# Gate and up of the last feed-forward's second half as seven block products of fp32 sums

## The chip, the core and the metric

The kernel runs on one core of a Trainium2 chip. The metric is the device time of one launch in microseconds. Engines are called PE (TensorE: matmuls, with their weight loads), DVE (VectorE), ACT (ScalarE), POOL (GpSimd) and SP (SyncE, which issues the transfers).

## What is computed

One inference step of a decoder with two layers, for a prompt of 1024 tokens and a sample group of 8 tokens that share all weights. D_MODEL is 1024, D_FF is 2816. Cut to what matters here:

```python
def swiglu(h, w_gu, w_down):
    gate, up = jnp.split(h @ w_gu, 2, axis=-1)
    return (jax.nn.silu(gate) * up) @ w_down

# for each layer l (a mixer of its own in each):
h = h + rmsnorm(mix, g[1])
h = h + rmsnorm(swiglu(rmsnorm(h, g[2]), w_gu[l], w_down[l]), g[3])
# after the last layer h is the output: y_prompt (1, 1024, 1024), y_sample (8, 1, 1024)
```

All data are fp32.

## The kernel before

Activations lie with the model dimension on the 128 partitions and tokens along the free dimension. The tokens are worked in two halves, `g` = 0 (512 prompt tokens) and `g` = 1 (512 prompt tokens and the 8 of the sample group, 520). A matmul of half 1 covers 260 tokens, so that its result fits a PSUM bank of 512 fp32; the two quarters lie in the two banks of one `mm` buffer.

fp32 products are made of three matmuls in the type fp32r: each operand is split into a rounded part and the difference to it (`split_to` for activations, `split_w` for weights: a cast on ACT, then a subtraction on DVE), and hi*hi, hi*lo and lo*hi are added up in PSUM. `proj` (matmuls: line 264) does this for 128 output channels over `nk` blocks of 128 input channels. `split_w` loads up to 4 such blocks of weights at a time (256 KB), with the cast in line 250 and the subtraction in line 251.

The feed-forward `ffn.part(pi)` works on a group of 5, 5, 4, 4 and 4 of the 22 blocks of 128 hidden channels (columns, below). For each column: the gate projection (8 input blocks x 3 x 2 quarters = 48 matmuls in half 1), `silu` (a clamp on DVE, Exp, Ln, Exp on ACT, a product on DVE), the up projection (48), their product, and a split of it (lines 271 and 272). Then eight down projections over the group's columns follow, added to `R` by `evac_raw` (line 403). In the last group `sq_acc` adds up the squares of the result (lines 300 to 304).

The normed input of a feed-forward comes from `out_proj.finish`: a residual and its sum of squares, `rstd_from` (a matmul with ones, line 293, then Ln and Exp), and `normed` (scale operations in line 310, then a split).

The order on each engine is not that of the source: a scheduler orders the instructions, and tiles come from pools with a fixed number of buffers, whose reuse waits for the last reader. `weave` fixes only the order in which streams are handed to it. Pools that matter here: `wraw` (5 raw weight tiles), `wspl` (5 split ones), `npool` (2; the tiles `n` of `sq_acc` and of `normed` in the last layer), `bpool` (7), `apool` (8), `cpool` (4), `xpool` (8 of each tag), and in PSUM `mmp` (2 x 2 banks), `smp` (3) and `nsp` (1).

The end of the kernel, around the change:

```python
    o1 = out_proj(1, 1, A, True)
    drain(o1.mm(b1.xo))
    weave((o1.finish(), 17), (f0.part(4), 8))
    f1 = ffn(1, 1, o1.x, True)
    weave((chain(f0.finish(False), store_y(0, f0.R), token_rows(1, o1.R)), 22), (chain(f1.part(0), f1.part(1)), 18))
    drain(f1.part(2), f1.part(3), f1.part(4), f1.finish_rows())
```

`f0` is the feed-forward of half 0 in the last layer, `f1` that of half 1. `store_y` and `token_rows` transpose results on PE through PSUM banks of `S()`; `first_half` and `finish_rows` turn the last result into rows of tokens and store them (Ln in line 525, Exp in line 526).

Of the kernel before, what the change touches and what calls it, by code (L numbers as in the profile page):

```python
# [8 lines left out]
F32 = mybir.dt.float32  # L9
# [8 lines left out]
P = 128  # L18
# [4 lines left out]
def tile_decoder(  # L23
# [38 lines left out]
    mmp = pool("mmp", 2, space=PSUM)  # L62
    smp = pool("smp", 3, space=PSUM)
    nsp = pool("nsp", 1, space=PSUM)
# [3 lines left out]
    def nm(s):  # L68
        uid[0] += 1
        return f"{s}_{uid[0]}"  # L70
# [9 lines left out]

    def NS():
        return nsp.tile([P, 512], F32, tag="ns", name=nm("ns"))
# [21 lines left out]
    def S():  # L104
        return smp.tile([P, 512], F32, tag="s", name=nm("s"))
# [209 lines left out]

    def wo_tiles(g):
        return [X(g) for _ in range(ND)]
# [89 lines left out]
    class out_proj:  # L407


        def __init__(self, g, l, store, last=False):  # L410
            self.g, self.l, self.store, self.x, self.last = g, l, store, [], last
# [11 lines left out]
        def finish(self):  # L423
            g, l = self.g, self.l
            rstd = rstd_from(self.acc, NG[g], 1.0 / D)
            acc = small([P, WID], tag="st", bufs=3)
            yield from residual(g, self.R, rstd, lambda k: gcol(l, 1, k), not self.last, acc, l == 0)
            r2 = rstd_from(acc, NG[g], 1.0 / D)
            yield
            yield from normed(g, self.R, r2, lambda k: gcol(l, 2, k), self.x, self.last)  # L430
# [23 lines left out]

    htok = []

    PARTS = [(0, 5), (5, 5), (10, 4), (14, 4), (18, 4)]

    class ffn:
# [4 lines left out]
        def part(self, pi):  # L464
# [18 lines left out]
            for m in range(ND):  # L483
                ps = proj(g, w_down[l], f0, nf, m * P, mids)
                evac_raw(g, self.R, ps, m, self.acc, pi == 0, last)
                if last and self.rows:
                    nc.scalar.activation(
                        self.R[m][:, :n], self.R[m][:, :n], AF.Copy, scale=gcol(l, 3, m)
                    )
                    if m == 3:  # L490
                        self.first_half()
# [11 lines left out]
        def first_half(self):  # L503
            self.yt = [xpool.tile([P, D], F32, tag="x0", name=nm("yT")) for _ in range(CH)]
            for c in range(CH):
                ps = S()
                for k in range(4):
                    nc.tensor.transpose(ps[:, k * P : (k + 1) * P], self.R[k][:, c * P : (c + 1) * P], ident)  # L508
                nc.scalar.copy(self.yt[c][:, :512], ps)
            self.ys = xpool.tile([P, D], F32, tag="x0", name=nm("yTs"))  # L510
            ps = S()
            for k in range(4):
                nc.tensor.transpose(ps[:NB, k * P : (k + 1) * P], self.R[k][:, G : G + NB], ident)
            nc.scalar.copy(self.ys[:NB, :512], ps[:NB, :])

        def finish_rows(self):

            ht, hsm = htok[0]
            g, R, acc = self.g, self.R, self.acc
            ps = NS()  # L520
            for c in range(CH):
                nc.tensor.matmul(ps[:, c : c + 1], acc[:, c * P : (c + 1) * P], ones[:, 0:1], start=True, stop=True)  # L522
            nc.tensor.matmul(ps[:NB, CH : CH + 1], acc[:, G : G + NB], ones[:, 0:1], start=True, stop=True)
            r = small([P, 8], tag="rr")
            nc.scalar.activation(r[:, :CH], ps[:, :CH], AF.Ln, scale=1.0 / D, bias=epsb)
            nc.scalar.activation(r[:, :CH], r[:, :CH], AF.Exp, scale=-0.5)
            rs = small([P, 8], tag="rr")
            nc.scalar.activation(rs[:NB, 0:1], ps[:NB, CH : CH + 1], AF.Ln, scale=1.0 / D, bias=epsb[:NB])
            nc.scalar.activation(rs[:NB, 0:1], rs[:NB, 0:1], AF.Exp, scale=-0.5)
            for c in range(CH + 1):  # L530
                prompt = c < CH
                n = P if prompt else NB
                yt, h = (self.yt[c], ht[c]) if prompt else (self.ys, hsm)
                rc = r[:, c : c + 1] if prompt else rs[:NB, 0:1]
                o = c * P
                pt = S()
                for k in range(4):
                    nc.tensor.transpose(pt[:n, k * P : (k + 1) * P], R[4 + k][:, o : o + n], ident)
                nc.vector.scalar_tensor_tensor(  # L539
                    yt[:n, :512], yt[:n, :512], rc, h[:n, :512], op0=ALU.mult, op1=ALU.add  # L540
                )
                nc.vector.scalar_tensor_tensor(  # L542
                    yt[:n, 512:], pt[:n, :], rc, h[:n, 512:], op0=ALU.mult, op1=ALU.add
                )
                if prompt:
                    t0 = g * G + c * P
                    nc.sync.dma_start(y_prompt[0, t0 : t0 + P, :], yt)
                else:
                    nc.sync.dma_start(y_sample.rearrange("b o d -> (b o) d"), yt[:NB])
                yield  # L550
# [689 lines left out]
```

## Time and profile before

| | us |
|---|---|
| median of 3 runs | 2550.11 |
| lowest and highest | 2548.95, 2551.8 |
| the profiled execution | 2551.36 |
| its span in the trace | 2549.6 |
| mean granted TensorE clock | 0.996 of full speed |
| first gate/up matmul of `f1` in the trace | 2144.5 after the span's start |
| last matmul of line 264 | ends at about 2535.9 |

Times in the trace are counted from the start of the span. In a row of the timeline the first number is the start, the second the length; in a row of the groups the two numbers behind the bar are the busy time of all and the mean of one in ns. A row of the windows has the busy time of PE, its weight loads, DVE, ACT and POOL, each with the count of instructions, then the granted clock, the transfers' share and GB/s.

### The profile page before, as it was taken

What the parts mean: (1) busy time and instruction counts of PE and PEld (TensorE: products, weight loads), DVE (VectorE), ACT (ScalarE), POOL (GpSimd) and SP (SyncE); (2) the same over time, 40 slices, a digit from 0 to 9 for tenths busy, and PEclk for the clock granted to TensorE, in tenths of its full rate; (3) what the DMA queues carried; (4) which work ended last, traced back from release to release, by engine and by line L of the source; (5) the groups of instructions that cost most, each with busy time, mean ns of one, the idle gap of its engine ahead of it and who ended that gap; (6) DMA issues with size and microseconds to landing.
All of it is one profiled execution on the core that took longest, in us unless ns stands there. A gap on an engine that the chain in (4) does not pass through costs nothing. (4 is left out here: it accounts for less than half of the span.)

```text
span 2549.6 us, 40536 instructions
## 1 busy us (share of the span) xinstructions
PE 2518.9 (99%) x15653; PEld 2193.2 (86%) x15653; DVE 1557.2 (61%) x2714; ACT 1186.6 (47%) x2187; POOL 43.8 (2%) x59
## 2 busy tenths in 40 slices
PE   8999999999999999999999999999999999999998
PEld 6888898878877888999999989766776798999998
DVE  6666566654775677555544577667677558444445
ACT  6346543243443445555433455455555445443334
POOL 1000000000000000000000000011000000000000
PEclk9999999999999999999999999999999999999999
DMA  6352242233644445231333445453443244323332
GB/s 186 109 162 71 75 150 76 65 112 116 182 127 129 136 153 183 86 88 57 102 93 94 126 153 179 144 153 94 135 140 115 77 124 129 110 86 103 93 92 67
DMA packets 457708, 297.91 MB, mean 117 GB/s; under 512 B 17573, under 2 KB 422642, under 8 KB 457514
## 3 DMA queue, kind: packets, MB, share of 16 engines
q1 hardware_dynamic: 454954, 286.92, 37.6%
q0 software_dynamic: 2560, 8.39, 1.1%
q8 instruction: 123, 2.02, 0.3%
q14 instruction: 71, 0.58, 0.1%
HBM read 265.44 MB, written 29.80 MB: 116 GB/s over the span
## 5 line engine op out<-in xcount | busy, mean ns | idle before, releaser
L264 PE MATMUL mm<-x,ws 128*128 128x260 f32 (+1 forms) x10080 | 1668.4, 323 | 1.4 <-ACT x L355 1.3
L264 PEld LDWEIGHTS mm<-x,ws 128*128 128x128 f32 x10080 | 1443.1, 188 | 166.3 <-issue 29.2
L250 ACT CAST ws<-w 128x512 fp32r<-128x512 f32 (+1 forms) x800 | 475.5, 595 | 878.4 <-PE mm L264 801.3
L251 DVE TENSOR_TENSOR ws<-w,ws 128x512 fp32r<-128x512 f32 (+1 forms) x800 | 523.5, 657 | 324.0 <-ACT ws L250 314.6
L264 PE MATMUL mm<-m,ws 128*128 128x260 f32 (+1 forms) x3168 | 544.4, 326 | 0.1
L264 PEld LDWEIGHTS mm<-m,ws 128*128 128x128 f32 x3168 | 455.1, 189 | 53.9 <-issue 7.1
L403 DVE TENSOR_TENSOR r<-r,mm 128x520 f32<-128x520 f32 (+1 forms) x128 | 88.3, 690 | 99.2 <-PE mm L264 97.7
L281 DVE TENSOR_SCALAR t<-mm 128x512 f32<-128x512 f32 (+1 forms) x104 | 72.1, 693 | 102.5 <-PE mm L264 102.0
L474 DVE TENSOR_TENSOR t<-t,mm 128x512 f32<-128x512 f32 (+1 forms) x88 | 60.8, 691 | 117.2 <-PE mm L264 117.2
L285 DVE TENSOR_TENSOR t<-t,t 128x512 f32<-128x512 f32 (+1 forms) x88 | 61.1, 694 | 88.3 <-ACT t L284 88.1
L304 DVE TENSOR_TENSOR st<-st,n 128x512 f32<-128x512 f32 (+1 forms) x98 | 67.0, 690 | 6.9 <-ACT n L303 5.0
L272 DVE TENSOR_TENSOR m<-t,m 128x512 fp32r<-128x512 f32 (+1 forms) x88 | 61.0, 694 | 3.7 <-ACT m L271 1.6
L282 ACT ACTIVATE t<-t 128x512 f32<-128x512 f32 (+1 forms) x88 | 55.9, 635 | 14.9 <-DVE t L281 7.8
L271 ACT CAST m<-t 128x512 fp32r<-128x512 f32 (+1 forms) x88 | 54.8, 623 | 10.1 <-DVE t L474 2.8
L283 ACT ACTIVATE t<-t 128x512 f32<-128x512 f32 (+1 forms) x88 | 55.8, 635 | 2.6
L284 ACT ACTIVATE t<-t 128x512 f32<-128x512 f32 (+1 forms) x88 | 55.9, 635 | 2.4
L902 PEld LDWEIGHTS s<-a,a 128*128 128x128 f32 x448 | 53.4, 192 | 1.2
L902 PE MATMUL s<-a,a 128*128 128x64 f32 x448 | 53.2, 271 | 0.0
L1073 PE MATMUL s<-b,trir 128*128 128x512 f32 (+3 forms) x96 | 38.0, 397 | 7.6 <-DVE b L272 5.3
L731 POOL DMA_INDIRECT c<-in_cache_sb_k,pidx x16 | 16.2, 1015 | 1640.7 <-DVE x L272 790.4
L1037 DVE SCALAR_TENSOR_TENSOR b<-b,b 128x512 f32<-128x512 f32 (+3 forms) x48 | 26.7, 556 | 28.2 <-ACT b L1036 28.0
L1085 PE MATMUL s<-b,a 128*128 128x512 f32 (+3 forms) x96 | 41.6, 515 | 1.9 <-DVE b L1040 1.5
(298 smaller groups left out, 1940.2 us busy)
## 6 DMA issues: line engine op xcount, KB each, us to landing
w<-in_w_gu SPq DMA_DIRECT2D x352, 256.0 KB, 3.0
w<-in_w_down SPq DMA_DIRECT2D x160, 256.0 KB, 2.8
w<-in_w_in_a SPq DMA_DIRECT2D x80, 256.0 KB, 2.9
w<-in_w_o SPq DMA_DIRECT2D x64, 256.0 KB, 2.8
w<-in_w_mem_kv SPq DMA_DIRECT2D x32, 256.0 KB, 2.9
c<-in_cache_mem_k SPq DMA_DIRECT2D x16, 512.0 KB, 4.2
c<-in_cache_mem_v SPq DMA_DIRECT2D x16, 512.0 KB, 3.9
w<-in_w_kv SPq DMA_DIRECT2D x32, 256.0 KB, 3.1
```

Source lines behind the costliest of these rows:

```text
L250: nc.scalar.copy(ws[:, 0, :n, :], raw[:, :n, :])
L251: nc.vector.tensor_sub(ws[:, 1, :n, :], raw[:, :n, :], ws[:, 0, :n, :].bitcast(F32))
L264: nc.tensor.matmul(ps[:, a, : PW[g]], wt, xt[k][:, xi, o : o + PW[g]], start=(k == 0 and wi == 0), stop=(k == nk - 1 and wi == 2),)
L272: nc.vector.tensor_sub(dst[1], src, dst[0].bitcast(F32))
L281: nc.vector.tensor_scalar(sv(x, g), pv(ps, g), -44.0, None, op0=ALU.max)
L282: nc.scalar.activation(d, x[:, :n], AF.Exp, scale=-1.0)
L284: nc.scalar.activation(d, d, AF.Exp, scale=-1.0)
L285: nc.vector.tensor_mul(d, d, x[:, :n])
L304: nc.vector.tensor_add(acc[:, :n], acc[:, :n], t[:, :n])
L403: nc.vector.tensor_add(dst, dst, pv(ps, g))
L474: nc.vector.tensor_mul(sv(sg, g), sv(sg, g), pv(pu, g))
L902: nc.tensor.matmul(plv[:, hh, c, :], K_[:, hh, cs], rhs, start=True, stop=True)
```

## The change

`f1` gets a class of its own, `ffn_w`. For a column, gate and up (2 output blocks) times the two halves of the 8 input blocks (0 to 3 and 4 to 7) make a 2 x 2 block matrix of weights a11, a12, a21, a22, each 128 x 512 as stored; the activations, input halves times token quarters of 260, make another. Their product is formed from seven block products (Strassen's scheme in Winograd's form) in place of eight. The sums and differences of weights (s1 to s4, fp32) are made on POOL, four of 512 elements for a column; those of the activations (r1 to r4) on POOL in `normed_w`, once. Each of the seven weight operands is then split (`split`), in place of four tiles before. Partial results are added up in single PSUM banks, with copies between banks on ACT. Silu is one activation function in place of Exp, Ln, Exp. The PSUM pools are closed ahead of `f1` and replaced by `quads`, 4 tags of 2 single banks; `S()` and `NS()` then take turns in two of these tags. Twelve small matmuls with constants are put ahead of the first column, the split weights of the later groups also use `cpool`, their raw weights `apool`, and the rates of the last `weave` are 17 to 7. `first_half` and `finish_rows` become functions without a change.

```diff
+    banks = ctx.enter_context(ExitStack())
...
+    def Q(i):
+        return single[0].tile([P, 512], F32, tag=f"q{i}", name=nm("q"))
...
     def S():
+        if single:
+            turn[0] += 1
+            return Q(3 * (turn[0] % 2))
...
+    def normed_w(R, rstd, gc, ops):
+        n, h = NG[1], PW[1]
+        xs, yt = {}, []
+        for k in range(4):
+            t0, t1 = N(), N()
+            for t, kk in ((t0, k), (t1, k + 4)):
+                nc.vector.scalar_tensor_tensor(
+                    t[:, :n], R[kk][:, :n], gc(kk), rstd[:, :n], op0=ALU.mult, op1=ALU.mult
+                )
+            x0, x1 = X(1), X(1)
+            split_to((x0[:, 0, :h], x0[:, 1, :h]), t0[:, :h])
+            split_to((x1[:, 0, :n], x1[:, 1, :n]), t1[:, :n])
+            yield
...
+            r1, r2, r3, r4 = B(), B(), B(), B()
+            nc.gpsimd.tensor_tensor(r1[:, :h], t0[:, h:n], t0[:, :h], op=ALU.subtract)
+            nc.gpsimd.tensor_tensor(r2[:, :h], t1[:, h:n], r1[:, :h], op=ALU.subtract)
+            nc.gpsimd.tensor_tensor(r3[:, :h], t1[:, h:n], t0[:, h:n], op=ALU.subtract)
+            nc.gpsimd.tensor_tensor(r4[:, :h], t1[:, :h], r2[:, :h], op=ALU.subtract)
+            zo = (k % 2) * h
+            for r, d, o in ((r1, x0, h), (r2, y, 0), (r3, y, h), (r4, z, zo)):
+                nc.scalar.copy(d[:, 0, o : o + h], r[:, :h])
+                nc.gpsimd.tensor_tensor(
+                    d[:, 1, o : o + h], r[:, :h], d[:, 0, o : o + h].bitcast(F32), op=ALU.subtract
+                )
...
+    def gate_up_w(l, f, ops, spl, whole):
...
+        a11, a12, a21, a22 = raw
+        s1, s2, s3, s4 = B(), B(), B(), B()
+        for d, x, y, op in (
+            (s1, a21, a22, ALU.add), (s2, s1, a11, ALU.subtract), (s3, a11, a21, ALU.subtract),
+            (s4, a12, s2, ALU.subtract),
+        ):
+            nc.gpsimd.tensor_tensor(d, x, y, op=op)
+
+        def split(src):
+            w = spl()
+            nc.scalar.copy(w[:, 0, :], src)
+            nc.vector.tensor_sub(w[:, 1, :], src, w[:, 0, :].bitcast(F32))
+            return w
+
+        def product(ps, src, i, first=False):
+            w = split(src)
+            for k in range(4):
+                x = ops[k][i]
+                for wi, (wj, xi) in enumerate(((0, 0), (0, 1), (1, 0))):
+                    nc.tensor.matmul(
+                        ps[:, :h], w[:, wj, k * P : (k + 1) * P], x[:, xi, :],
+                        start=(first and k == 0 and wi == 0), stop=(k == 3 and wi == 2), skip_group_check=True,
+                    )
+
+        pa, pb, pc, pd = (Q(i) for i in range(4))
+        product(pa, a11, 0, True)
+        nc.scalar.copy(pb[:, :h], pa[:, :h])
+        product(pd, s1, 4, True)
+        product(pb, s2, 5)
+        nc.scalar.copy(pc[:, :h], pb[:, :h])
+        product(pa, a12, 1)
+        sg = T()
+        nc.scalar.activation(sg[:, :h], pa[:, :h], AF.Silu)
+        product(pb, s3, 6)
+        up = T()
+        nc.scalar.copy(up[:, h:n], pd[:, :h])
+        gt = T()
+        nc.vector.tensor_add(gt[:, h:n], up[:, h:n], pb[:, :h])
+        product(pc, s4, 2)
+        nc.vector.tensor_add(gt[:, :h], up[:, h:n], pc[:, :h])
+        product(pb, a22, 3)
+        nc.scalar.activation(sg[:, h:n], gt[:, :h], AF.Silu)
+        nc.vector.tensor_mul(sg[:, :h], sg[:, :h], pb[:, :h])
+        nc.vector.tensor_mul(sg[:, h:n], sg[:, h:n], gt[:, h:n])
+        mt = M(F32R)
+        split_to((mt[:, 0, :n], mt[:, 1, :n]), sg[:, :n])
+        return mt
...
+    class ffn_w:
...
+        def spl(self):
+            self.n += 1
+            if pi_now[0] and self.n % 8 in (1, 4, 6):
+                return cpool.tile([P, 2, 512], F32R, tag="c", name=nm("ws"))
+            return wspl.tile([P, 2, 512], F32R, tag="ws", name=nm("ws"))
...
+            if pi == 0:
+                for i in (1, 2, 1, 2):
+                    ps = Q(i)
+                    for o in range(0, h, P):
+                        w = min(P, h - o)
+                        nc.tensor.matmul(
+                            ps[:, o : o + w], trir, cmpr[:, :w], start=(o == 0), stop=(o + w == h),
+                            skip_group_check=True,
+                        )
...
+            if last:
+                self.acc = small([P, WID], tag="st", bufs=3)
+                nc.scalar.preload_act_table_set("natural_log_exp_and_others")
...
-    o1 = out_proj(1, 1, A, True)
+    o1 = out_proj(1, 1, A, True, True)
     drain(o1.mm(b1.xo))
     weave((o1.finish(), 17), (f0.part(4), 8))
-    f1 = ffn(1, 1, o1.x, True)
-    weave((chain(f0.finish(False), store_y(0, f0.R), token_rows(1, o1.R)), 22), (chain(f1.part(0), f1.part(1)), 18))
+    banks.close()
+    single.append(ctx.enter_context(tc.tile_pool(name="quads", bufs=2, space=PSUM)))
+    f1 = ffn_w(1, o1.x)
+    weave((chain(f0.finish(False), store_y(0, f0.R), token_rows(1, o1.R)), 17), (chain(f1.part(0), f1.part(1)), 7))
```

In the down projections of `ffn_w` each quarter has a bank of its own and an evacuation of 260 elements, where one of 520 stood before.

More of the change, by code (lines that the diff above doesn't have):

```diff
@@ L407, in tile_decoder, with __init__ @@
     class out_proj:
[L410 to L411 removed]
+        def __init__(self, g, l, store, last=False, seven=False):
+            self.g, self.l, self.store, self.x, self.last, self.seven = g, l, store, [], last, seven
         def mm(self, xo, m0=0, m1=ND):
@@ L429, in finish @@
             yield
-            yield from normed(g, self.R, r2, lambda k: gcol(l, 2, k), self.x, self.last)
+            if self.seven:
+                yield from normed_w(self.R, r2, lambda k: gcol(l, 2, k), self.x)
+            else:
+                yield from normed(g, self.R, r2, lambda k: gcol(l, 2, k), self.x, self.last)
     def token_rows(g, R):
@@ L453, in token_rows @@
         htok.append((ht, hs_))
+    def gate_up_w(l, f, ops, spl, whole):
+        h, n = PW[1], NG[1]
+        raw = []
+        for m0 in (f * P, DFF + f * P):
+            if whole:
+                r = apool.tile([P, 2, 4, P], F32, tag="a", name=nm("w"))
+                ts = [r[:, 0], r[:, 1]]
+            else:
+                ts = [wraw.tile([P, 4, P], F32, tag="w", name=nm("w")) for _ in range(2)]
+            for i, r in enumerate(ts):
+                k0 = 4 * i
+                nc.sync.dma_start(
+                    r, w_gu[l][k0 * P : (k0 + 4) * P, m0 : m0 + P].rearrange("(k p) m -> p k m", p=P)
+                )
+                raw.append(r.rearrange("p k m -> p (k m)"))
+        a11, a12, a21, a22 = raw
[42 more added lines that the diff above has]
+        return mt
@@ L501, in finish, with first_half @@
                 yield
[L503 to L510, printed above, removed]
+    def first_half(self):
+        self.yt = [xpool.tile([P, D], F32, tag="x0", name=nm("yT")) for _ in range(CH)]
+        for c in range(CH):
@@ L511, in first_half @@
             ps = S()
             for k in range(4):
[L513 to L550, printed above, removed]
```

104 lines of the change are left out of this document (100 added, 4 removed).

## The prediction

> **What bounds the kernel now.** I read the page first (engine shares and the chain that ended last), then the windows over the last 600 us, then the timeline of PE there, and last the groups by form for prices.
>
> ```profile
> span 2549.6 us, 40536 instructions
> ...
> PE 2518.9 (99%) x15653; PEld 2193.2 (86%) x15653; DVE 1557.2 (61%) x2714; ACT 1186.6 (47%) x2187; POOL 43.8 (2%) x59
> ...
> PE 20%; DVE 0%; ACT 0%; DVEq 0%; issue 0%
> ```
> ```profile
> 2300.00:2400.00 100.00, 100.00 (x838) 100.00 (x837) 47.06 (x73) 33.70 (x57) 0.00 (x0) 1.00 0.35 100
> ```
> PE is never idle in the stage that changes: matmuls and weight loads fill this window, at the full granted clock, while DVE is busy 47%, ACT 34% and Pool not at all. A matmul taken out here is time gained, until another engine's work for it no longer fits beside the matmuls that stay.
>
> ```profile
> 2123.49 21.12 PE L264 MATMUL mm<-m,ws 128*128 128x512 f32 x90
> 2144.54 3.94 PE L264 MATMUL mm<-x,ws 128*128 128x260 f32 x31
> ...
> 2326.17 46.08 PE L264 MATMUL mm<-x,ws 128*128 128x260 f32 x384
> 2372.08 23.20 PE L264 MATMUL mm<-m,ws 128*128 128x260 f32 x192
> ```
> The changed stage begins at 2144.54, without a gap behind the last down projection of the prompt's first half. In steady state a group of four columns takes 384 gate/up matmuls from 2326.17 to 2372.08: 45.91 / 384 = 119.6 ns each, 11.48 us for a column of 96; its down projections take 23 us.
>
> **What goes.** `gate_up_w` has seven products of 12 matmuls, 84 for 96, each of the same 128x260 form, with one weight load each as before. A column takes 84 x 119.6 ns = 10.05 us of PE, a product 1.44 us. Over 22 columns 264 matmuls go: **-31.6 us**. The down projections keep theirs, and the 12 small matmuls ahead of the first column lie in a wait (below).
>
> **Does the other work fit into 10.05 us a column?** Prices:
>
> ```profile
> L251 DVE TENSOR_TENSOR ws<-w,ws 128x512 fp32r<-128x512 f32 x221 | 152.1, 690 | 77.3 <-ACT ws L250 75.6
> L250 ACT CAST ws<-w 128x512 fp32r<-128x512 f32 x221 | 137.1, 621 | 265.1 <-PE mm L264 256.7 <-issue 5.7 <-DMA w<-in_w_gu 1.0
> ...
> L272 DVE TENSOR_TENSOR m<-t,m 128x520 fp32r<-128x520 f32 x22 | 15.4, 699 | 2.3 <-ACT m L271 1.6
> ...
> L250 ACT CAST ws<-w 128x128 fp32r<-128x128 f32 x22 | 6.6, 298 | 34.5 <-PE mm L264 34.4
> L251 DVE TENSOR_TENSOR ws<-w,ws 128x128 fp32r<-128x128 f32 x22 | 6.4, 291 | 29.9 <-ACT ws L250 29.8
> ```
> ```profile
> 2102.67 1.29 DVE L251 TENSOR_TENSOR ws<-w,ws 128x512 fp32r<-128x512 f32 x2
> 2103.87 0.70 DVE L304 TENSOR_TENSOR st<-st,n 128x520 f32<-128x520 f32 x1
> ```
> ```profile
> 2107.08 0.64 ACT L303 ACTIVATE n<-a 128x520 f32<-128x520 f32 x1
> 2107.63 0.62 ACT L284 ACTIVATE t<-t 128x512 f32<-128x512 f32 x1
> ```
> Back to back, a full-width DVE operation occupies its engine 0.60 us (two in 1.20) and an ACT one 0.55, less than their durations. Between the 128- and 512-wide rows, a 260-wide one lasts about 0.43 (DVE) or 0.41 us (ACT) and occupies some 0.33. DVE per column: seven weight differences and one of the result, 8 x 0.60, and four 260-wide operations, 1.3: 6.1 us. ACT: eight casts, 8 x 0.55, three copies out of PSUM and two Silu, 5 x 0.33: 6.1 us. Both fit. Nor does the order within a column stall: each copy between banks has one product (1.44 us) between the end of its source and the product that adds onto it, and needs 0.41; the casts of the next column stand on ACT right behind the copies of this one, some seven products before their use. Loads on SP's queue stay four of 256 KB a column.
>
> ```profile
> masks.py:199 POOL TENSOR_SCALAR_AFFINE_SELECT ident<-ident 128x128 f32<-128x128 f32 x1 | 0.3, 284 | 0.0
> ...
> L201 POOL TENSOR_SCALAR_AFFINE_SELECT bdm<-ones 8x8 f32<-8x8 f32 x1 | 0.2, 182 | 0.0
> ```
> ```profile
> w<-in_w_gu SPq DMA_DIRECT2D x352, 256.0 KB, 3.0
> ```
> Pool is the new engine, and the trace has none of its fp32 sums of two inputs. The nearest rows have one: (284 - 182) / 120 = 0.85 ns an element, so with some 0.17 fixed 0.6 us for 512 and 0.39 for 260; that is the lower bound, twice the whole for the second input, 1.2 and 0.78, the upper. Twice per element alone is 1.04 and 0.61. I take 1.2 and 0.65, since the rows read half of what these read. Four sums a column are 2.4 to 4.8 us. In the first group, where a column uses four of `wraw`'s five buffers, the third load waits for the column before to finish s4: 3.0 us of load and 4.8 of sums, 7.8 < 10.05. So Pool fits; it bounds the first group from (10.05 - 3.0) / 4 = 1.76 us a sum. In the other groups two columns' loads lie ahead.
>
> **The start of the stage is where time is lost.** `normed_w` puts a chain through three engines ahead of the first products, and its t0 and t1 take both buffers of `npool`, which the squares of the running down projection (`sq_acc`) use too. Pool gives them back only after r2, r3 and r4. On DVE the next pair of scale operations then waits for Pool and for two squares; behind them on DVE stand the evacuations of the down projection.
>
> ```profile
> 2129.19 0.75 DVE L310 SCALAR_TENSOR_TENSOR n<-a,par,st 128x520 f32<-128x520 f32 x1
> ...
> 2134.28 0.68 DVE L403 TENSOR_TENSOR r<-r,mm 128x512 f32<-128x512 f32 x1
> ...
> 2145.53 0.68 DVE L403 TENSOR_TENSOR r<-r,mm 128x512 f32<-128x512 f32 x1
> ```
> The first pair can start at 2129.2 as before. The second waits for the square of m = 3, evacuated at 2134.28: 0.68, square 0.64, sum 0.69: about 2136.6. From then a period is two scale operations 1.4, three Pool sums 1.95, a cast 0.41, a square 0.64 and a sum 0.69: 5.1 us, so 2141.8; the last pair waits a little longer (the square of m = 7, evacuated at 2145.5): 2147.9. The evacuations m = 4 to 7 come up to 2 us late, which two accumulators absorb. In the order of the built program PE's second instruction of the stage is then the sum of squares of the first half, which waits for DVE's last one, at 2149.1. PE stands from 2145.2 to there; product 1 ends at 2150.9. Product 2 and 3 need s1 and s2, which stand on Pool behind the last k step: its scale operation ends at 2148.6, then r1 0.65, a copy 0.41, and one difference, r2, r3, r4 at 0.65 each, s1 1.2: 2153.4; with the ACT queue (Ln, copy, Exp and the cast) the weights of product 2 come at 2154.8. Two more differences and s2: 2155.9, cast 0.62: product 3 starts at 2156.5. The last ten matmuls of product 2, ten of product 3 and four products follow: 2156.7 + 2.4 + 5.75 = 2165. Without a gap the column would end at 2144.5 + 10.05 = 2154.6. Loss **+10.4 us**; with the lower Pool prices the same chain ends at 2161: +6.4.
>
> ```profile
> 2537.00:2538.00 1.00, 0.00 (x0) 0.00 (x0) 0.61 (x1) 0.97 (x2) 0.00 (x0) 1.00 0.00 0
> ...
> 2541.00:2542.00 1.00, 0.64 (x3) 0.64 (x4) 1.00 (x3) 0.00 (x0) 0.00 (x0) 0.57 0.00 0
> ```
> At the kernel's end the granted clock falls (column before the last two) some 4 us after PE's first gap. Two gaps of 4 us here may do the same: 12 to 24 matmuls at half speed are +1.4 to 2.9 us; between none and 3 I take **+1.5**.
>
> **Smaller terms.** The transposes now take turns in banks of the products; each waits in ACT's or DVE's queue for a copy (0.6 us), in some three places: **+2** (0 to 4). At the end, Silu has replaced the activation tables. In the built order the preload in the last group has been lost: a table load stands ahead of Ln, and another between Ln and Exp of `finish_rows`.
>
> ```profile
> 0.79 1.28 ACT L121 ACT_TABLE_LOAD   x1 [0.79 <-PEq L1228]
> ```
> ```profile
> 2539.36 0.26 ACT L525 ACTIVATE rr<-ns,epsb 128x4 f32<-128x4 f32 x1 [1.24 <-PE ns L523]
> ...
> 2539.67 0.20 ACT L526 ACTIVATE rr<-rr 128x4 f32<-128x4 f32 x1
> ```
> The first fits into ACT's idle 1.24 us ahead of Ln; the second's 1.28 us is on the path, with 0.1 for a last evacuation in two halves: **+1.4**. The Silu table's load in the first column lies on ACT, with its casts well ahead.
>
> **Sum.** Against the profiled execution's 2551.36 us: -31.6 + 10.4 + 1.5 + 2 + 1.4 = -16.3. The median is 2550.11, so the result is about **2534 us**. A measurement here tells 0.2%, 5.1 us, from no change.
>
> **Rivals.** (1) DVE and Pool shut each other out. Nothing in the trace speaks to it: in the window above Pool is idle. If a DVE operation with two SBUF inputs cannot run during a Pool sum, a column needs 4.8 of Pool, 6.1 of DVE: 10.9 for 10.05. In later groups the work lies ahead by some seven products (10 us) and DVE has 23 us of down projection with 8 x 0.60 + 16 x 0.33 = 10 us of work, so 4 x 0.85 us is made up. In the first group DVE also has the first half's residual, 16 full operations, 10 us, and four copies, 2.4: 5 x 10.9 + 12.4 = 67 for 50 us of products and 6 of transposes: up to 11 us lost, and some 3 in the starting chain. It gives 2538 to 2548. The Trainium skill (SBUF — State Buffer, Who interferes with whom) says just this: a DVE instruction with two SBUF inputs contends with a Pool instruction that reads SBUF, and the later one blocks until the first is done. No run here has shown it yet; by that rule this rival is the forecast.
>
> (2) Slower than before: the sums themselves set the pace. If waiting for DVE stretches a Pool sum's turn, each sum holding DVE too, so that DVE needs x us a column, a later group needs 4x + 10 us of DVE against 63 of PE: it decides from x = 13.2, that is 1.75 us for each sum's turn instead of 1.2. At x = 14.5 the 22 columns lose 1.3 us each, 29 us: with the rest 2563. The idle share of DVE (half of the window) speaks against it.
>
> (3) The start costs less: Pool at the one-input price and no loss of clock: -31.6 + 6.4 + 0 + 1 + 1.4 = -22.8, 2527. The change does what it says in any case: 84 matmuls of the same form stand in the built order for each column.
>
> **Chances.** Forecast, 2530 to 2539: 0.50. Rival 1, 2538 to 2548: 0.28. Rival 3, 2524 to 2530: 0.13. Rival 2, above 2555: 0.09. The range is 2525 to 2548. Faster by over 0.2% (below 2545): 0.50 + 0.13 + most of rival 1, 0.85; the rest of rival 1, 0.06, is the same; slower 0.09.
>
> **What would show it.** Right: PE's gate/up row at 120 ns a matmul with 1848 of them, a column in about 10.05 us in the later groups; PE waiting some 4 us for a DVE sum at the first half's squares and about 4 more for ACT's cast of s1 and s2; Pool's 512-wide sums at about 1.2 us apart; a table load between Ln and Exp. Wrong: weight differences longer than 0.69 us where Pool runs (rival 1), PE waits for casts in the groups after the first (rival 2), or no gap at the start.

## The result: slower, 2580.4 us for 2549.8

The changed kernel took 2580.41 us in the median of 4 runs (2576.31 to 2580.95), the kernel before 2549.78: a ratio of 1.0115, 95% interval 1.0098 to 1.0133. The forecast was 2534 us, in a range of 2525 to 2548.

The profiled execution of the changed kernel took 2576.31 us. Its page, the parts that answer to those shown of before:

```profile
span 2574.6 us, 40457 instructions
...
PE 2512.3 (98%) x15401; PEld 2171.5 (84%) x15401; DVE 1650.6 (64%) x2832; ACT 1223.9 (48%) x2326; POOL 211.4 (8%) x179
...
PE q L543 6%; PE q L621 4%; PE mm L276 4%; DVE ws L535 1%; DVE r L440 0%; DVE t L567 0%; POOL y L355 0%; DMA w<-in_w_gu 0%; DVE r L434 0%; DVE ws L263 0%; POOL b L530 0%; ACT ws L534 0%; DVE t L561 0%; POOL b L348 0%; PE q L493 0%
```

PE has lost its matmuls (252 fewer are on record: 264 gone, the twelve small ones added), yet its busy time fell by 6.6 us only while the span grew by 25: time was lost to idle PE, and the matmuls that are left became dearer. In the lines of the changed kernel 543 are the gates' matmuls, 621 the down projections', 276 those of `proj`, 530 the weight sums, 534 and 535 the casts and differences of split weights, 348 to 355 the sums of the normed operands.

PE's timeline from the last down products of half 0 on (start, length, what it did, and in brackets what ended its idle time):

```profile
2146.44 7.37 PE L276 MATMUL mm<-m,ws 128*128 128x512 f32 x24 [3.44 <-ACT x L283]
2156.47 1.50 PE L601 MATMUL q<-cmpr,trir 128*128 128x128 f32 x12 [2.66 <-DVE r L453]
2157.83 0.37 PE L543 MATMUL q<-x,ws 128*128 128x260 f32 x1
2160.85 2.07 PE L305 MATMUL q<-st,ones 128*128 128x512 f32 x2 [2.65 <-DVE st L316]
2161.93 3.30 PE L543 MATMUL q<-x,ws 128*128 128x260 f32 x11
2167.91 0.51 PE L543 MATMUL q<-x,ws 128*128 128x260 f32 x2 [2.67 <-ACT ws L534]
2170.47 0.80 PE L543 MATMUL q<-y,ws 128*128 128x260 f32 x2 [2.05 <-ACT ws L534]
...
2197.07 2.97 PE L543 MATMUL q<-y,ws 128*128 128x260 f32 x12 [5.55 <-DVE t L561]
```

The waits at the start are those that the prediction named (the squares, then the casts of s1 and s2), but they are not all: the last down projection waits before them, and a wait of 5.55 us stands in the middle of the second column. The windows of 30 us around the start (PE, its weight loads, DVE, ACT, POOL, then the granted clock), first of before, then of the changed kernel:

```profile
2140.00:2170.00 30.00, 30.00 (x228) 28.39 (x227) 29.96 (x50) 16.74 (x28) 0.00 (x0) 1.00 0.34 98
2170.00:2200.00 30.00, 30.00 (x253) 30.00 (x252) 13.79 (x21) 12.85 (x21) 0.00 (x0) 1.00 0.24 70
```
```profile
2140.00:2170.00 30.00, 16.99 (x65) 12.59 (x64) 22.22 (x25) 13.86 (x31) 26.34 (x29) 0.80 0.08 30
2170.00:2200.00 30.00, 22.84 (x155) 22.24 (x156) 28.57 (x35) 13.93 (x27) 17.01 (x11) 0.84 0.42 123
2200.00:2230.00 30.00, 27.33 (x205) 26.92 (x204) 23.97 (x33) 16.09 (x33) 12.67 (x8) 0.90 0.28 85
```

PE is idle for 13 of the first 30 us and 7 of the next, and the clock falls to 0.80 to 0.90 in the mean, where before it was 1.00. Cut into its stages by the end of each stage's last matmul, the time from the sum of squares in `o1.finish` (line 305, before 293) to the end is, with the experiments beside it (us):

| stage | before | after | e8 | e5 | s1 | e7 |
|---|---|---|---|---|---|---|
| start of the span to the sum of squares | 2121.1 | 2125.0 | 2117.5 | 2117.8 | 2122.6 | 2120.1 |
| to the end of half 0's last down projection | 23.6 | 28.8 | 29.7 | 28.8 | 23.6 | 23.6 |
| first group: gates, down projections | 58.4, 33.5 | 84.1, 35.8 | 83.3, 35.6 | 74.6, 35.1 | 66.8, 35.1 | 62.6, 33.3 |
| second group | 60.2, 29.6 | 55.9, 29.3 | 56.2, 29.6 | 51.1, 28.7 | 51.5, 28.7 | 54.3, 28.7 |
| third | 45.9, 23.0 | 42.9, 24.3 | 42.8, 23.5 | 41.4, 23.0 | 41.1, 23.0 | 41.0, 23.4 |
| fourth | 45.9, 23.1 | 41.9, 24.3 | 41.8, 24.6 | 41.1, 23.3 | 41.2, 23.3 | 41.7, 23.3 |
| fifth | 45.9, 25.8 | 41.6, 25.8 | 42.1, 25.8 | 41.0, 25.8 | 40.9, 25.8 | 41.0, 25.8 |
| tail | 13.7 | 14.8 | 14.8 | 14.8 | 14.8 | 14.8 |
| all from the sum of squares | 428.6 | 449.6 | 449.9 | 428.7 | 415.7 | 413.5 |

(e8: other addresses; e5: weight sums on DVE too; s1: no sums of the normed operands either; e7: the first group in plain products. All are told below.)

### The profile page after: what moved, and what is told of

Its sections match the earlier page's. It is cut to its first block, busy times and chain, and to the rows that moved or that the text cites. A ratio compares the mean times of both kernels' runs of the same rounds, so it can differ in the third digit from the quotient of the medians.

```text
span 2574.6 us, 40457 instructions
## 1 busy us (share of the span) xinstructions
PE 2512.3 (98%) x15401; PEld 2171.5 (84%) x15401; DVE 1650.6 (64%) x2832; ACT 1223.9 (48%) x2326; POOL 211.4 (8%) x179
## 3 DMA queue, kind: packets, MB, share of 16 engines
q0 software_dynamic: 2560, 8.39, 1.1%
## 5 line engine op out<-in xcount | busy, mean ns | idle before, releaser
L276 PE MATMUL mm<-x,ws 128*128 128x260 f32 (+1 forms) x7968 | 1424.0, 334 | 0.7 <-ACT x L405 0.7
L276 PEld LDWEIGHTS mm<-x,ws 128*128 128x128 f32 x7968 | 1189.7, 188 | 174.4 <-issue 28.3
L262 ACT CAST ws<-w 128x512 fp32r<-128x512 f32 x712 | 420.4, 591 | 715.4 <-PE mm L276 595.9
L263 DVE TENSOR_TENSOR ws<-w,ws 128x512 fp32r<-128x512 f32 x712 | 470.3, 663 | 290.7 <-ACT ws L262 282.0
L276 PE MATMUL mm<-m,ws 128*128 128x512 f32 (+1 forms) x2112 | 415.7, 348 | 3.4 <-ACT x L283 3.4
L276 PEld LDWEIGHTS mm<-m,ws 128*128 128x128 f32 x2112 | 327.6, 189 | 57.3 <-issue 7.1
L543 PE MATMUL q<-x,ws 128*128 128x260 f32 x1056 | 142.7, 288 | 2.7 <-ACT ws L534 2.7
L543 PEld LDWEIGHTS q<-x,ws 128*128 128x128 f32 x1056 | 135.6, 194 | 3.9 <-ACT ws L534 2.9
L621 PE MATMUL q<-m,ws 128*128 128x260 f32 x1056 | 130.6, 283 | 2.1 <-ACT m L283 1.1
L621 PEld LDWEIGHTS q<-m,ws 128*128 128x128 f32 x1056 | 127.7, 188 | 3.8 <-ACT m L283 1.5
L535 DVE TENSOR_TENSOR ws<-w,ws 128x512 fp32r<-128x512 f32 x66 | 66.1, 1003 | 15.6 <-ACT ws L534 15.4
L283 ACT CAST m<-t 128x512 fp32r<-128x512 f32 (+1 forms) x88 | 54.8, 622 | 25.0 <-DVE t L566 17.3
```

The lines of the kernel that those rows point to most:

```text
L262: nc.scalar.copy(ws[:, 0, :n, :], raw[:, :n, :])
L263: nc.vector.tensor_sub(ws[:, 1, :n, :], raw[:, :n, :], ws[:, 0, :n, :].bitcast(F32))
L276: nc.tensor.matmul(ps[:, a, : PW[g]], wt, xt[k][:, xi, o : o + PW[g]], start=(k == 0 and wi == 0), stop=(k == nk - 1 and wi == 2),)
L283: nc.scalar.copy(dst[0], src)
L535: nc.vector.tensor_sub(w[:, 1, :], src, w[:, 0, :].bitcast(F32))
L543: nc.tensor.matmul(ps[:, :h], w[:, wj, k * P : (k + 1) * P], x[:, xi, :], start=(first and k == 0 and wi == 0), stop=(k == 3 and wi == 2), ...
```

## The experiments

**Which sums cost (e1, e2, e3).** The theory was that a DVE operation with two SBUF inputs and a Pool operation shut each other out; the rival that the chain ahead of the first products, with the low clock behind its gaps, is the loss.

```diff
 e1:
-            nc.gpsimd.tensor_tensor(d, x, y, op=op)
+            nc.vector.tensor_tensor(d, x, y, op=op)
 e2, for r1 to r4 and for the four differences behind them:
-            nc.gpsimd.tensor_tensor(r1[:, :h], t0[:, h:n], t0[:, :h], op=ALU.subtract)
+            nc.vector.tensor_tensor(r1[:, :h], t0[:, h:n], t0[:, :h], op=ALU.subtract)
 e3: both
```

> The four weight sums of each column on DVE, the sums of the normed operands still on Pool. Theory A (a DVE operation with two SBUF inputs and a Pool operation shut each other out, and this is what stretched the first group): DVE then needs 6.1 + 4 x 0.6 = 8.5 us of a column's 10.05; the differences ws<-w last about 0.7 instead of 1.0 us, the gates of the first group take 62 to 72 us instead of 86.5, and the time falls from 2580 to 2556 to 2566. Rival B (the chain ahead of the first products and the low clock behind its gaps cost the time; the stretched operations are a symptom): the chain is as before, the first column ends at most 3 us earlier, the time is 2573 to 2580. Rival C (DVE becomes the bound with the sums): the groups after the first get slower than 42 us for four columns.

> The sums of the normed operands and their differences on DVE, the weight sums still on Pool. Theory A: only the chain ahead of the first products gets shorter (its periods of 10.2, 6.8 and 8.9 us fall to 5 to 7), the first column ends 8 to 12 us earlier; the columns behind it stay in lock step with Pool (differences still about 1.0 us): the time is 2566 to 2572. Rival B: most of the loss goes with the chain, and the later columns of the first group fall to 11 us each: 2550 to 2560.

> All sums on DVE, none on Pool. Theory A: both losses go, 2536 to 2550: the first group's gates take 55 to 65 us and no DVE operation with two SBUF inputs lasts more than 0.7 us for 512 elements. Rival C (DVE is the bound): DVE has 8.5 us a column, and in the first group the residual and the sums of the normed operands too, 5 x 8.5 + 12 + 13 = 68 us for 50 of products; then the first group stays above 70 us and the time is 2555 to 2570.

Measured: e1 2561.18 us (ratio to before 1.0033, 1.0021 to 1.0046), e2 2579.94 (1.0109, 1.0092 to 1.0126), e3 2561.72 (1.0037, 1.0023 to 1.0052). The weight sums on Pool are worth 19 us, as theory A had it, though the gates of the first group still took 74.1 us. The sums of the normed operands gain next to nothing in time by going to DVE. Both theories missed e2; theory A missed e3, which lies in rival C's range, but with some 10 us of it spent ahead of the stage (below). By the stage alone, from the sum of squares to the end, the profiles have 449.6 us for the changed kernel, 428.9 for e1, 445.7 for e2 and 429.4 for e3. The timeline of PE in e3 tells why:

```profile
2133.37 19.13 PE L276 MATMUL mm<-m,ws 128*128 128x512 f32 x80
2161.55 3.94 PE L276 MATMUL mm<-m,ws 128*128 128x512 f32 x10 [9.06 <-DVE ws L263]
```

and DVE there, the last step of the chain:

```profile
2155.95 0.42 DVE L284 TENSOR_TENSOR x<-n,x 128x260 fp32r<-128x260 f32 x1
...
2160.48 0.41 DVE L355 TENSOR_TENSOR y<-b,y 128x260 fp32r<-128x260 f32 x1
2160.82 0.68 DVE L263 TENSOR_TENSOR ws<-w,ws 128x512 fp32r<-128x512 f32 x1
```

On DVE the sums are short (0.42 us for 260 elements), but they stand in front of a weight difference of half 0's running down projection, which PE waits 9.06 us for. So the loss moves: in e3 half 0's last down projection ends 34.6 us behind the sum of squares (28.8 in e1), and the gates of the first group take 69.0 us (74.1).

**The lock, seen in the changed kernel.** DVE and Pool during the second column (timelines of both):

```profile
2188.69 0.68 DVE L535 TENSOR_TENSOR ws<-w,ws 128x512 fp32r<-128x512 f32 x1
2189.29 0.68 DVE L440 TENSOR_TENSOR r<-r,ht 128x512 f32<-128x512 f32 x1
2189.89 1.78 DVE L434 SCALAR_TENSOR_TENSOR r<-r,par,st 128x512 f32<-128x512 f32 x1
2191.59 1.75 DVE L535 TENSOR_TENSOR ws<-w,ws 128x512 fp32r<-128x512 f32 x1
2193.26 1.75 DVE L440 TENSOR_TENSOR r<-r,ht 128x512 f32<-128x512 f32 x1
2194.94 1.74 DVE L535 TENSOR_TENSOR ws<-b,ws 128x512 fp32r<-128x512 f32 x1
2196.60 0.41 DVE L561 TENSOR_TENSOR t<-t,q 128x260 f32<-128x260 f32 x1
```
```profile
2189.50 1.62 POOL L530 TENSOR_TENSOR b<-w,w 128x512 f32<-128x512 f32 x1 [4.36 <-DVE ws L535]
2191.20 1.60 POOL L530 TENSOR_TENSOR b<-b,w 128x512 f32<-128x512 f32 x1
2192.75 1.71 POOL L530 TENSOR_TENSOR b<-w,w 128x512 f32<-128x512 f32 x1
2194.43 1.70 POOL L530 TENSOR_TENSOR b<-w,b 128x512 f32<-128x512 f32 x1
```

From the moment at which Pool starts, the two take turns: an operation of one and one of the other every 1.7 us, DVE's own 0.6 us and some 1.1 for the sum. PE waits 5.55 us for the 260-wide addition (line 561) at the end of that queue; itself it lasts 0.41 us. One of its inputs lies in PSUM, and all 22 of these additions lasted 0.41 to 0.43 us, the one at 2179.09 us in the middle of a Pool sum (2178.88 to 2180.31) too. The page SBUF — State Buffer of the Trainium skill (Who interferes with whom) states this: a DVE instruction with two SBUF inputs contends with a Pool instruction that reads SBUF, and the later one fully blocks. The trace agrees, in both directions: the DVE operations of 0.68 and 0.74 us become 1.74 to 1.78 beside Pool, and Pool's sums 1.60 to 1.71, where the shortest on record took 1.26. With the weight sums moved, in the kernel of e5, the differences are back at the price of before (groups by form, the changed kernel first, then e5; the last number of the second field is the mean of one in ns):

```profile
L535 DVE TENSOR_TENSOR ws<-b,ws 128x512 fp32r<-128x512 f32 x88 | 82.0, 941 | 26.8 <-ACT ws L534 25.6
L535 DVE TENSOR_TENSOR ws<-w,ws 128x512 fp32r<-128x512 f32 x65 | 64.9, 999 | 15.6 <-ACT ws L534 15.4
```
```profile
L535 DVE TENSOR_TENSOR ws<-b,ws 128x512 fp32r<-128x512 f32 x88 | 59.9, 686 | 11.4 <-ACT ws L534 11.1
L535 DVE TENSOR_TENSOR ws<-w,ws 128x512 fp32r<-128x512 f32 x65 | 44.7, 687 | 10.2 <-ACT ws L534 9.7
```

**The lock by itself (b4).** Four Pool sums behind each column of the kernel before, read by nobody:

```diff
                 mids.append(mt)
+                if self.rows:
+                    for _ in range(4):
+                        nc.gpsimd.tensor_tensor(
+                            B()[:, :512], mt[:, 0, :512].bitcast(F32), mt[:, 1, :512].bitcast(F32), op=ALU.add
+                        )
```

> The kernel before with four Pool sums of two inputs of 512 elements added behind each column of the last feed-forward's second half; nobody reads what they write. The disputed port by itself: by theory A DVE's operations with two SBUF inputs of the next column wait for a Pool operation each or the reverse, so that the differences ws<-w of the stage go from 690 to 850 or more ns and a Pool sum lasts 1.1 to 1.8 us, while DVE (half busy in the plain kernel) hides nearly all of it: 0 to +4 us. Rival (no lock; the long operations of the changed kernel came from waiting on each other's data): differences stay at 690 ns, sums at 1.1 us.

Measured: 2551.63 us, ratio 1.0001 (0.9992 to 1.0011). The groups of DVE and POOL in its stage:

```profile
L251 DVE TENSOR_TENSOR ws<-w,ws 128x512 fp32r<-128x512 f32 x125 | 102.3, 820 | 41.5 <-ACT ws L250 40.2
L403 DVE TENSOR_TENSOR r<-r,mm 128x520 f32<-128x520 f32 x31 | 21.5, 694 | 26.0 <-PE mm L264 25.7
...
L384 DVE SCALAR_TENSOR_TENSOR r<-r,par,st 128x512 f32<-128x512 f32 x8 | 7.8, 1001 | 0.0
```
```profile
L480 POOL TENSOR_TENSOR b<-m 128x512 f32<-128x512 f32 x88 | 129.0, 1498 | 622.6 <-DVE m L272 615.7 <-PE mm L264 6.8
```

and the same of DVE in the kernel before:

```profile
L251 DVE TENSOR_TENSOR ws<-w,ws 128x512 fp32r<-128x512 f32 x125 | 86.2, 691 | 43.9 <-ACT ws L250 42.4
L403 DVE TENSOR_TENSOR r<-r,mm 128x520 f32<-128x520 f32 x31 | 21.6, 695 | 32.5 <-PE mm L264 31.9
...
L384 DVE SCALAR_TENSOR_TENSOR r<-r,par,st 128x512 f32<-128x512 f32 x8 | 5.8, 742 | 0.0
```

The differences went from 691 to 820 ns in the mean (theory A had 850 or more) and the residual's scaling from 742 to 1001, while the additions that read PSUM stayed at 694. So the lock is there although DVE reads nothing that Pool writes; and it costs nothing as long as nobody waits for DVE or for the sums. In the changed kernel both stand ahead of PE's next product. e1 and e5 take away the blocking and Pool's longer sums at once; what each is worth alone was not measured.

**Does the blocking cost in the later groups too (p1)?** In the kernel with the plain first group (e7, below) the weight sums of the other four groups were put back on Pool, with the edit of e1 the other way round.

> The kernel with the plain first group, and the weight sums of the other four groups on Pool again. The prediction held that groups after the first make up the blocking, since DVE idles in their down products: then 2534 to 2538. Theory A, with the four later groups and their down products of the stride experiments (all sums on Pool against sums on DVE), 286 against 276 us: 2543 to 2549.

Measured: 2543.40 us (0.9972, 0.9962 to 0.9983), against 2535.38 for e7, in theory A's range. So eight of the 19 to 21 us are lost behind the first group's gates, where the prediction had them made up.

**More buffers for the chain (e4).**

```diff
-            t0, t1 = N(), N()
+            t0, t1 = T(), T()
```

> Engines as in the changed kernel; the two normed tiles of each step come from the pool of the gate's temporaries (three buffers, free at that time) and not from the two that the squares of the running down projection use. Theory A: the chain is bound by Pool's and DVE's blocking, so the periods fall by only 1 to 3 us each; the time is 2570 to 2578. Rival B' (the two buffers, as the prediction's chain had it, set the periods): the wait for the squares goes, the first column ends 6 to 10 us earlier, 2562 to 2570.

Measured: 2581.78 us (ratio 1.0116, 1.0099 to 1.0133). Neither expectation held. The first and the last pair of scale operations (line 337) stand 25.5 us apart, 26.0 in the changed kernel: the two buffers, on which the prediction's chain was built, do not set its pace by themselves.

**Time lost ahead of the change (b0, b1, b2).** In the profiles of the changed kernel and of e1 to e4 the sum of squares (line 305), ahead of which nothing of the change is executed, comes 4 to 10 us later than before, and one group of matmuls is slower. The scheme's operand `y` is a tile of 520 columns under the tag of half 0's `x` tiles, which have 512. A tag's buffers all get the size of its widest tile, so the stride of eight `x` buffers went from 4096 to 4160 bytes. b0 is the kernel before once more; b1 and b2 change its addresses alone:

```diff
 b1 (b2: 2 * NG[1] + 16, and bpool 6 buffers in place of 7):
-        self.ys = xpool.tile([P, D], F32, tag="x0", name=nm("yTs"))
+        self.ys = xpool.tile([P, 2 * NG[1]], F32, tag="x0", name=nm("yTs"))[:, :D]
```

> The kernel before once more, for a second profile of it. In all five profiles with the change, the last 2000 us of unchanged code ahead of it take 4 to 10 us longer than in the profile of before, and 128x512 matmuls of mm<-x,ws have a mean of 248 to 249 ns instead of 245. Theory D (the addresses of these x tiles, which the change moved, make it): this profile shows 245 ns again and the sum of squares ahead of the stage at 2121 us, within 2. Rival (chip or day): 248 to 249 ns here too.

> The kernel before, with one tile at its very end declared 4160 instead of 4096 bytes wide, which gives all eight buffers of that tag a stride of 4160 bytes, as in the changed kernel; no instruction is added or changed. Theory D (addresses): mean 248 to 249 ns for the 128x512 matmuls of mm<-x,ws, some 3360 of them and so up to 11 us, of which waits take up a part: 2556 to 2562. Rival (something else in the changed kernel slows the code ahead of it): 2549 to 2554 as before.

> The kernel before with that tag at a stride of 4224 bytes, a multiple of 128 but not of 256 (one buffer of another pool given up). If a multiple of 128 is enough, it runs as before, 2548 to 2555; if the step that matters is 256, half the tiles are off it and the time is 2554 to 2560, with a mean between 398 and 402 ns.

Measured: b0 2551.00 in one run; b1 2560.42 (1.0039, 1.0024 to 1.0054); b2 2562.29 (1.0044, 1.0027 to 1.0060). The largest group of PE's first 2120 us in before, b0, b1, b2, the changed kernel and e8 (below):

```profile
L264 PE MATMUL mm<-x,ws 128*128 128x512 f32 x3356 | 822.6, 398 | 1.3 <-ACT x L355 1.3
```
```profile
L264 PE MATMUL mm<-x,ws 128*128 128x512 f32 x3357 | 824.3, 399 | 1.1 <-ACT x L355 1.1
```
```profile
L264 PE MATMUL mm<-x,ws 128*128 128x512 f32 x3331 | 827.8, 401 | 1.4 <-ACT x L355 1.4
```
```profile
L264 PE MATMUL mm<-x,ws 128*128 128x512 f32 x3307 | 825.6, 402 | 1.2 <-ACT x L355 1.2
```
```profile
L276 PE MATMUL mm<-x,ws 128*128 128x512 f32 x3339 | 829.8, 401 | 0.7 <-ACT x L405 0.7
```
```profile
L276 PE MATMUL mm<-x,ws 128*128 128x512 f32 x3360 | 823.4, 398 | 0.7 <-ACT x L405 0.7
```

The matmuls that read these buffers last 401 to 402 ns in place of 398 to 399 (counts differ because some records are missing; there are 3360 of them). They overlap, so the expectations count the busy time for each, 245 to 246 against 248 to 250 ns by these rows. From the start of one to the start of the next, back to back, the traces have 227 ns in the median in before, b0, e5 and e8, and 232 in b1, b2 and the changed kernel; the mean is 3.4 to 4.0 ns longer, 11.6 to 13.5 us over 3360. b1 alone, with not one instruction changed, is 8.7 us slower than before. In its profile the sum of squares comes at 2126.7 us, in b2's at 2132.5 (2121.1 before, 2120.7 in b0), and from there to the end all four take 428.5 to 428.7 us. The rival (chip or day) falls with b0; a stride that is a multiple of 128 (b2) is not enough (its expectation for a step of 256 had at most 2560 us).

**The addresses mended (e8, e5).** e8 is the changed kernel, e5 is e1, both with a stride of 4352 bytes, paid for with a buffer of `bpool`:

```diff
-        return xpool.tile([P, 2, NG[1]], F32R, tag="x0", name=nm("y"))
+        return xpool.tile([P, 2, NG[1] + 24], F32R, tag="x0", name=nm("y"))
-    bpool = pool("bpool", 7)
+    bpool = pool("bpool", 6)
```

> The changed kernel, all sums on Pool, with the buffers at a stride of 4352 bytes and one buffer of another pool given up: the addresses alone. Theory D: the mean of mm<-x,ws 128x512 goes from 401 to 398 ns and the time from 2580 to 2567 to 2573; the stage itself stays as it was (449 us from the sum of squares to the end). Rival (addresses and lock overlap, since PE waits anyway): 2575 to 2580.

> Weight sums on DVE as in the first experiment, and the buffers at a stride of 4352 bytes, a multiple of 256 (one buffer of another pool is given up for it). Theory D with 256 bytes as the step that matters: the mean is 245 ns again and the time falls from 2561 to 2550 to 2555. Theory D with a coarser step (512 or 4096): the mean stays at 247 to 249, 2556 to 2562. Rival (not the addresses): 2559 to 2563.

Measured: e8 2570.34 (1.0077, 1.0060 to 1.0094), e5 2549.59 (0.9993, 0.9983 to 1.0002). The group is back at 398 ns in both, and e8's stage is as long as the changed kernel's (449.9 and 449.6 us), the buffer given up included: 10.1 us of the loss lie ahead of the change and go with the addresses, as theory D had it (e5 is half a us better than it had).

**The sums of the normed operands left out (s1).** e5 without r1 to r4 and their splits; the products that need them read the plain operands.

> The kernel of the 4352-byte stride with weight sums on DVE; the sums of the normed operands and their splits are left out (the products that need them read the plain operands, so that the outputs are not the reference's). Theory A (the sums of the operands stand ahead of the first product and cost some 20 us): f0's last down products end 23 to 25 us behind the sum of squares instead of 28.8, the first column some 12 us behind them instead of 26.5, and the time falls from 2549.6 to 2528 to 2536. Rival (the first group loses its time to DVE's weight sums and splits beside the residual, not to the chain): 2541 to 2549.

Measured: 2537.75 us (0.9946, 0.9928 to 0.9964), 11.8 below e5 and between the two expectations. Half 0's down projection no longer waits (23.6 us from the squares to its end, as before), and the first column ends at 2163.5, 17.3 us behind it instead of 26.5. So the operand sums cost 12 us, of the 20 that theory A gave them (13.1 by the stage). The other waits of PE stay:

```profile
2147.11 1.50 PE L587 MATMUL q<-cmpr,trir 128*128 128x128 f32 x12 [0.93 <-DVE r L439]
...
2165.82 11.85 PE L529 MATMUL q<-x,ws 128*128 128x260 f32 x84 [1.85 <-DVE ws L521]
2178.64 10.32 PE L529 MATMUL q<-x,ws 128*128 128x260 f32 x84 [0.98 <-DVE ws L521]
```

**The first group in plain products (e6, e7).** The scheme in the other four groups only. The operand sums are made on DVE from the residual scaled once more: r2 to r4 beside the first group's gates, r1, which takes the place of a plain operand, beside its down projections. Weight sums on DVE, stride 4352. e6 lacked the twelve small matmuls that the scheme's first accumulations need.

```diff
+        def plain(self, f0, nf):
...
+                if 1 <= j <= 4:
+                    w.three(j - 1)
...
+                if m % 2:
+                    w.first(m // 2)
+                    yield
+            banks.close()
+            single.append(ctx.enter_context(tc.tile_pool(name="quads", bufs=2, space=PSUM)))
```

> As the one before, and the first group of five columns in plain products of the banks of before; the scheme in the other four groups only. The sums of the normed operands are made on DVE while the first group runs, from its residual scaled once more, so nothing of them stands ahead of the first product. It saves 17 x 12 = 204 matmuls, 24.4 us, instead of 264. Theory A (what was lost lay in the start and in the first group): about 24 us less than before with 1.4 for the tail, 2524 to 2532, plus up to 10 us if the addresses still cost. Rival C (DVE with the sums bounds the first group): its gates take over 65 us instead of 58.3, 2535 to 2550.

> As the one with the plain first group, with the twelve small matmuls with constants put back ahead of the scheme's first column; the earlier one lacked them, and its accumulating products then started on banks in another state. They take 2.5 us at most and PE is not waiting there: 2530 to 2534. Theory A says that what is left against before is 24.4 us saved, 1.4 lost in the tail, and DVE's extra work hidden in the first group; if DVE or the pacing of the two streams cost, the first group's gates and down products take more than the 58.3 and 33.5 us of before.

Measured: e6 2530.57 us, in theory A's range; e7, the whole kernel, 2535.38 us, ratio 0.9936 (0.9919 to 0.9953): faster than the kernel before and the changed one. Its windows at the place where the changed kernel lost its time:

```profile
2140.00:2170.00 30.00, 30.00 (x231) 28.55 (x231) 29.97 (x52) 17.34 (x30) 0.00 (x0) 1.00 0.24 68
2170.00:2200.00 30.00, 29.58 (x250) 29.31 (x249) 29.83 (x60) 16.13 (x33) 0.00 (x0) 1.00 0.49 160
```

PE is fed and the clock stays at 1.00, while DVE is as full as it can be (29.97 and 29.83 of 30 us); PE waits 0.42 us in all. e7 was above its expectation: of 24.4 us saved in matmuls 15.7 arrive. The table has the rest: 54.3 us in the second group for 5 x 10.05 = 50.3 (the twelve small matmuls and the wait ahead of them, 2.2 us, stand on the path there), 41.0 to 41.7 for 40.2 in each later one, and 4.2 more in the first group's gates, with `store_y`'s transposes, which stood in its down projections before; those of `token_rows` have moved out of the second group's gates.

## Why the prediction was wrong, step by step

By medians the 46 us between forecast and result come apart so (the median of before moved between 2549.8 and 2552.2 from round to round, so a share is good to some 2 us): changed kernel 2580.4; addresses 10.1 (to e8); weight sums on Pool 20.7 (to e5); operand sums 11.8 (to s1); what is left of s1, 2537.8, above 2551.4 - 31.6 + 1.4 = 2521.2 is 16.6. Against the last two stood the prediction's 10.4 + 1.5 + 2 = 13.9 us. That is 45.3 us; the rest is about the 1.2 us between the profiled execution, from which this sum goes, and the median.

- **What goes, -31.6: right in size, not all of it arrives.** 84 matmuls a column run; a group of four columns takes 41.0 to 41.4 us where DVE makes the sums (e5), 45.9 before, forecast 40.2. Of the 1 us a group that is missing, 0.2 to 0.6 goes to short waits for DVE (line 561).
- **DVE 6.1 and Pool 4.8 us a column, both "fit": the step that failed most.** Pool's price was about right (the turn above leaves 1.1 us for a sum of 512, the shortest took 1.26, taken was 1.2), but "So Pool fits" counted the two side by side where they exclude each other: in the first group its sums stood 1.7 us apart, not 1.2. The weight sums on Pool cost 20.7 us.
- **Rival 1 was the right mechanism, sized wrongly, and given 0.28.** Its sign, weight differences longer than 0.69 us, is in the rows: 0.94 and 1.00. It counted 11 us for the first group, 3 for the start and none later, on the ground that the work lies seven products ahead and DVE idles in the down projections. From e8 to e5 the first group's gates fall by 8.7 us, and all behind them by 11.5; p1 shows 8 us for the later groups alone. Idle time in the down projections did not make up waits in the gates; whether more buffers for split weights would let it was not tried.
- **Rival 2 (the sums set the pace, 1.75 us a turn): true in parts of the first group,** where the turns took 1.7 us, and not in the later groups.
- **The start, +10.4: mis-sized, and its mechanism not borne out.** The order of waits came as described. But the periods of the chain, counted from the scale operations (line 337), were about 10, 7 and 9 us, 26.0 in all, not 7, 5 and 6; and it delayed half 0's down projection by 5.3 us, for which the sum had nothing ("which two accumulators absorb"). What sets its pace stays open: other buffers (e4) left 25.5 us, the weight sums off Pool (e1) 26.0, and all sums off Pool (e3) 27.0, so that neither the two buffers of `npool` nor Pool's blocking is the whole reason. Only where the operand sums do not stand ahead of it (s1, e7) does the down projection end on time.
- **The clock, +1.5: too small.** Between 2148 and 2216 us the granted clock fell to 0.50 five times, among gaps of 1.1 to 5.6 us; behind the wait of 3.2 us in the second group it did not. The records of the changed kernel between 2110 and 2260 us have PE busy for 21 us at half clock, which is 10.6 us of full-speed work lost (worked out in the same way 6.9 in e5, 3.3 in s1, none in e7). What of it would have been idle time anyway was not measured.
- **The transposes, +2: not seen as such.** In e5 and s1 PE waits once for a copy between them, 1.5 us; in the changed kernel it does not.
- **The tail, +1.4: right.** The tail takes 14.8 us, 13.7 before. The second table load stands between Ln and Exp (ACT's timeline):

```profile
2563.21 0.26 ACT L708 ACTIVATE rr<-q,epsb 128x4 f32<-128x4 f32 x1
2563.37 0.24 ACT L711 ACTIVATE rr<-q,epsb 8x1 f32<-8x1 f32 x1
2563.63 1.28 ACT L709 ACT_TABLE_LOAD   x1
2564.92 0.20 ACT L709 ACTIVATE rr<-rr 128x4 f32<-128x4 f32 x1
```

- **No term at all for code that the change does not touch.** The prediction took some 2100 us of it as given; it cost 10.1 us more by addresses.

## What to carry to other kernels

Work that is moved to Pool is not free if DVE works on two SBUF inputs beside it: count both on one clock wherever someone waits for either, and measure the pair, not the engine. Work ahead of a stage's first matmul is paid twice, in idle PE and in the low clock behind the gap; it was cheaper to leave the first group as it was than to speed it up. And when a tile of another size joins a pool's tag, look at the addresses of all tiles of that tag: a profile row of an untouched line that changes by 1% is worth following.

## What was not expected of the hardware

- A 128x512 matmul of fp32r data takes 398 to 399 ns when its moving operand lies in buffers at a stride of 4096 or 4352 bytes, and 401 to 402 at 4160 or 4224; before and b1 differ in the addresses alone. Matmuls of 260 columns stayed at 286 ns in all of these kernels, at whatever address. What the address does inside the chip stays open; only these four strides were tried, and the buffers behind them in memory moved along (by 512 to 2048 bytes).
- The granted clock in the records is either 1.0 or 0.50, and within the span a stretch at 0.50 lasts 3.4 us or a multiple of it (3.41 and 6.83 us in the changed kernel); a window's 0.80 is a mix of the two. The page TensorE: Matmul & The Clock Gate of the Trainium skill (Part 1) has the same two levels and the same window.
- The multiply-and-scale form with a per-partition factor (`SCALAR_TENSOR_TENSOR r<-r,par,st`) is blocked by Pool like a two-input sum: 742 to 1001 ns in b4.
